# Hybrid decoder layer on one Trainium2 core: adaLN products as row products on VectorE, GpSimd and ScalarE, separate weight tiles for the output projection, and the next norm begun inside the input projection

## The chip, the cores and the metric

The kernel runs on one core of one Trainium2 chip. The metric is the device time of one execution in microseconds; for the kernel before it is the median of three runs. Engines are named as the profile names them: PE is TensorE's matmul and PEld its weight load, DVE is VectorE, ACT is ScalarE, POOL is GpSimd, SP is SyncE, whose queue issues nearly all DMAs of this kernel.

## The reference

One layer, batch 1, 2048 tokens, width 1024, all in float32:

```python
mod = jax.nn.silu(c) @ w_ada[layer] + b_ada[layer]
shift1, scale1, gate1, shift2, scale2, gate2 = jnp.split(mod, N_MOD, axis=-1)
h = modulate(rmsnorm(x, norm1_w[layer]), shift1, scale1)
x = x + gate1[:, None, :] * hybrid_mixer(h, ...)
h = modulate(rmsnorm(x, norm2_w[layer]), shift2, scale2)
x = x + gate2[:, None, :] * swiglu(h, w_gate_up[layer], w_down[layer])
...
return rmsnorm(x, final_norm_w)
```

`modulate(h, shift, scale)` is `h * (1 + scale) + shift`. `hybrid_mixer` makes one input projection (queries, keys, values, a gate z, the convolution's channels and dt), runs sliding-window attention on one half of the heads and a chunked state-space scan (SSD, 128 tokens in a chunk) on the other half, and joins both in one output projection. `w_ada` is 1024 x 6144; `mod` therefore has 48 groups of 128 numbers, and each group needs a 1024 x 128 piece of `w_ada`, 512 KB.

## The kernel before, in words

**Tiling.** Activations lie transposed: 128 channels on the partitions, 512 tokens along a row, so a block of 512 tokens is 8 tiles of 128x512. There are four blocks, 0 to 3. Every float32 matmul operand is split into a high and a low part of a faster format; `mm3` (lines 210 to 213) then issues three matmuls for each product. A weight tile is loaded by `weight` (lines 199 to 208): a DMA into one of five `raw` buffers, the high part by ACT (L204), the low part by POOL (L207) into one of six `w` pairs.

**Stages.** `first_norm` normalises block 0. Then, for each block b, `in_proj(b)` projects (queries, keys and values, eight convolution columns from `wx`, z), `norm1(b+1)` makes the operands of the next block, and for b = 1 and 2 `out_proj(b-1)` projects the mixer's output of the block before. Attention and SSD of a block are generators (`attentions`, `ssds`) that are kept in a list `sides`, and `beside` runs 1.6 steps of them for each step of the main generator. Before `out_proj(b-1)` stands `finish(ssd_of[b-1])`, which runs the list until that block's SSD is written: the output projection needs it. Attention of a block and its SSD follow each other, four steps of 128 tokens each, and the SSD carries a state from chunk to chunk. Later come the gate-up products of block pair 0 (`quads`, with a Strassen-like scheme of seven products), `down(0)` and `down(1)` with `out_proj(2)` and `out_proj(3)` beside them, the second pair's `quads`, and `down(2)` and `down(3)`.

**adaLN.** `ada(i, ...)` makes group i of `mod`. It loads 128x1024 numbers of `w_ada` (tile `mo` in the first norm, `aw` with a single buffer later) and issues eight matmuls (L142) that contract 128 input channels each with a column of silu(c) that is doubled to two columns (`csil`, 128x8x2). A matmul of this type is recorded as two weight loads and two passes, so eight matmuls are 16 records. DVE then adds the bias from PSUM. The first norm needs 16 groups (scale1 and shift1); `rest_of_ada` makes the other 32, one at each step of `beside` from `in_proj(1)` on. `first_norm` interleaves the groups with `modulated` (lines 242 to 248): DVE scales (L244), ACT makes the high part with the shift (L246), DVE the low part (L247); each of the eight results is one contraction step of the first queries' projection.

**Order.** The program is written as above, and a scheduler that estimates durations then orders the instructions of each engine. An engine takes its instructions strictly in that order; only the waits decide when each starts. SP's queue too is in order, so a DMA that waits for a free buffer holds the DMAs behind it.

**The final norm.** `down(b)` keeps eight residual tiles `x2` of its block (L807 loads them from `mid`), adds the products into them (L826), and leaves a generator that applies the final norm (L849, in place in `x2`) and stores (L850). It is run inside the next block's `down`, after columns 0 and 2. The residual tiles are a pool of eight, with three spare tiles `s` for even blocks.

## Time and profile before

| | |
|---|---|
| median of three runs | 2494.17 us (2491.22 to 2494.92) |
| the profiled execution | 2498.42 us, of which the span is 2496.6 us |
| mean granted TensorE clock | 0.958 |
| DVE, ACT, POOL busy | 55%, 42%, 58% of the span |
| DMA | 336.08 MB, mean 135 GB/s |

The chain that ended last lies on PE for 65% of the span, on DVE for 5%, on DMA for 2%. The program's stages, by the first and last instructions of their lines: first norm and queries of block 0 to 98.6 us, attention of block 0 from 120 to 305 us, its SSD to 408 us, `in_proj(1)` to 365 us, `out_proj(0)` from 395 us, attention of block 1 to 597 us and its SSD to 694 us, first `quads` from about 870 us, `down(0)` from about 1400 us, second `quads` from about 1750 us, `down(3)` from 2359 us to the end.

The views by stage give start:end, the length, then each engine's busy microseconds with its number of instructions, the granted clock, the DMA engines' busy share and GB/s. The timeline gives start, length, engine, line, operation, tiles, and in brackets the idle time before an instruction with what ended it. "Idle" in the groups' view is again time before the group's instructions, with the releaser behind it.

### The profile page before, as it was taken

To read this page: it belongs to the slowest core of one execution; us is meant where nothing else is said; L and a number is where in the kernel's file an instruction comes from. 1 tells how busy PE (TensorE), PEld (TensorE's weight loads), DVE (VectorE), ACT (ScalarE), POOL (GpSimd) and SP (SyncE) were. 2 spreads that over 40 slices of the span, in tenths; PEclk is the share of its full clock that TensorE was granted. 3 is DMA by queue.
4 is the path that set the end of the run, shared out by engine and by line. 5 is a ranking of instruction groups with operands and counts; after the bars stand their busy time and mean duration, and the time that the engine had idled before them with its cause. 6 is when DMAs were issued, how large, how long until landed. Compare 5 with 4: busy or idle time off the path is not lost.

```text
span 2496.6 us, 34763 instructions
## 1 busy us (share of the span) xinstructions
PE 2365.6 (95%) x11966; PEld 1995.6 (80%) x11966; DVE 1375.8 (55%) x2404; ACT 1060.5 (42%) x2155; POOL 1444.2 (58%) x1404
## 2 busy tenths in 40 slices
PE   7998998999689979999999999998999999999797
PEld 7988897899579858888888788876888888878576
DVE  5266455336644597665665535369555554554445
ACT  2366544446346643444443434334333333333332
POOL 2565563557546678655687544547666666643433
PEclk8899997999789979999999999999999999999998
DMA  6446555554444432222323555465242222263531
GB/s 217 130 150 192 180 175 176 193 171 146 125 156 148 130 107 91 81 73 85 99 87 95 180 172 187 154 222 162 89 141 76 81 86 87 76 198 101 186 117 61
DMA packets 208671, 336.08 MB, mean 135 GB/s; under 512 B 20592, under 2 KB 66672, under 8 KB 208496
## 3 DMA queue, kind: packets, MB, share of 16 engines
q1 hardware_dynamic: 207344, 332.83, 41.7%
q8 instruction: 94, 1.54, 0.3%
q10 hardware_dynamic: 1152, 1.05, 0.1%
q14 instruction: 81, 0.66, 0.1%
HBM read 266.69 MB, written 67.11 MB: 134 GB/s over the span
## 4 chain that ended last, share of the span: by engine, by line
PE 65%; DVE 5%; DMA 2%; issue 1%; ACT 1%; POOL 1%; SPq 0%; DVEq 0%; ACTq 0%
PE d L748 8%; PE d L746 8%; PE d L747 8%; PE d L211 8%; PE d L212 8%; PE d L213 8%; PE am L211 1%; PE am L213 1%; PE am L212 1%; PE am L748 1%; PE st L748 1%; PE sm L748 1%; PE sm L746 1%; PE am L746 1%; PE am L747 1%
## 5 line engine op out<-in xcount | busy, mean ns | idle before, releaser
L207 POOL TENSOR_TENSOR w<-raw,w 128x512 fp32r<-128x512 f32 (+1 forms) x224 | 295.9, 1327 | 255.4 <-ACT w L204 232.3
L692 ACT ACTIVATE w<-raw 128x512 fp32r<-128x512 f32 x308 | 193.6, 630 | 442.7 <-PE d L213 200.7
L747 PE MATMUL d<-b,w 128*128 128x512 f32 x924 | 368.2, 399 | 7.5 <-DVE b L720 7.1
L746 PE MATMUL d<-b,w 128*128 128x512 f32 x924 | 368.6, 399 | 0.3 <-DVE t L771 0.2
L748 PE MATMUL d<-b,w 128*128 128x512 f32 x924 | 367.9, 399 | 0.0
L211 PE MATMUL d<-a,w 128*128 128x512 f32 (+1 forms) x720 | 280.2, 396 | 28.2 <-DVE x L826 21.5
L212 PE MATMUL d<-a,w 128*128 128x512 f32 (+1 forms) x720 | 283.4, 394 | 4.4 <-DVE a L687 4.4
L213 PE MATMUL d<-a,w 128*128 128x512 f32 (+1 forms) x720 | 282.5, 392 | 0.0
L693 POOL TENSOR_TENSOR w<-s,w 128x512 fp32r<-128x512 f32 x132 | 189.4, 1435 | 156.8 <-ACT w L692 156.6
L693 POOL TENSOR_TENSOR w<-raw,w 128x512 fp32r<-128x512 f32 x88 | 123.4, 1403 | 197.3 <-ACT w L692 193.3
L693 DVE TENSOR_TENSOR w<-raw,w 128x512 fp32r<-128x512 f32 x220 | 191.6, 871 | 57.8 <-ACT w L692 52.3
L204 ACT ACTIVATE w<-raw 128x512 fp32r<-128x512 f32 (+1 forms) x224 | 139.8, 631 | 182.2 <-PE d L213 128.9
L747 PEld LDWEIGHTS d<-b,w 128*128 128x128 f32 x924 | 175.5, 190 | 47.9 <-DVE b L720 8.0
L746 PEld LDWEIGHTS d<-b,w 128*128 128x128 f32 x924 | 175.0, 189 | 40.4 <-DVE t L714 0.7
L826 DVE SCALAR_TENSOR_TENSOR x<-d,mod,x 128x512 f32<-128x512 f32 (+1 forms) x164 | 117.7, 722 | 162.5 <-PE d L213 150.4
L748 PEld LDWEIGHTS d<-b,w 128*128 128x128 f32 x924 | 175.0, 189 | 38.6
L211 PE MATMUL d<-w,hl 128*128 128x256 f32 (+1 forms) x640 | 187.6, 296 | 1.3 <-ACT hl L246 1.3
L212 PE MATMUL d<-w,hl 128*128 128x256 f32 (+1 forms) x640 | 187.6, 294 | 0.0
L213 PE MATMUL d<-w,hl 128*128 128x256 f32 (+1 forms) x640 | 187.1, 295 | 0.4 <-DVE hl L247 0.4
L211 PEld LDWEIGHTS d<-a,w 128*128 128x128 f32 x720 | 136.8, 190 | 62.3 <-issue 19.7
L212 PEld LDWEIGHTS d<-a,w 128*128 128x128 f32 x720 | 137.2, 191 | 37.4 <-DVE a L687 7.1
L213 PEld LDWEIGHTS d<-a,w 128*128 128x128 f32 x720 | 136.9, 190 | 31.5 <-issue 0.5
(312 smaller groups left out, 5654.4 us busy)
## 6 DMA issues: line engine op xcount, KB each, us to landing
raw<-in_wgu_dram SPq DMA_DIRECT2D x176, 256.0 KB, 2.7
raw<-in_wd_dram SPq DMA_DIRECT2D x176, 256.0 KB, 2.7
act<-t SPq DMA_DIRECT2D x88, 256.0 KB, 2.1
t<-act SPq DMA_DIRECT2D x88, 256.0 KB, 4.4
t<-in_xT_dram SPq DMA_DIRECT2D x80, 256.0 KB, 3.8
raw<-in_wx_dram SPq DMA_DIRECT2D x64, 256.0 KB, 3.0
aw<-in_wada_dram SPq DMA_DIRECT2D x32, 512.0 KB, 3.8
raw<-in_wo_dram SPq DMA_DIRECT2D x64, 256.0 KB, 2.7
```

The source lines that it names most:

```text
L204: nc.scalar.activation(hi, raw[:, :n], AF.Copy)
L207: eng.tensor_tensor(lo, raw[:, :n], hi.bitcast(F32), ALU.subtract)
L211: nc.tensor.matmul(out, ahi, bhi, start=first, stop=False)
L212: nc.tensor.matmul(out, ahi, blo, start=False, stop=False)
L213: mm3.last = nc.tensor.matmul(out, alo, bhi, start=False, stop=last)
L692: nc.scalar.activation(hi, x, AF.Copy)
L693: eng.tensor_tensor(lo, x, hi.bitcast(F32), ALU.subtract)
L746: nc.tensor.matmul(out, ahi, bhi, start=first and k == 0, stop=False, skip_group_check=True)
L747: nc.tensor.matmul(out, ahi, blo, start=False, stop=False, skip_group_check=True)
L748: mm3.last = nc.tensor.matmul(out, alo, bhi, start=False, stop=k == 3, skip_group_check=True)
L826: nc.vector.scalar_tensor_tensor(x, ps, gate2[:, c:c + 1], x, ALU.mult, ALU.add)
```

## The change

- `ada` no longer uses PE. `w_ada` is laid out with an output channel on each partition and the 1024 inputs along the row; silu(c), doubled, is broadcast to all partitions (`csil`, now 128x1024, from a new input `crow`). A group is then a product with `csil` and a sum along the row, half of which is taken (0.5). By default DVE does this in one instruction, `tensor_tensor_reduce`, that also adds the bias. For the eight shift groups of the first norm (`shared`) POOL multiplies (128x1024), ACT sums with its accumulator, and DVE adds the bias.
- `rest_of_ada` is started in step 4 of `in_proj(0)`, and not after it.
- `weight` takes an optional pool of its own: the output projection loads into two `rawo` buffers and two `wo` pairs instead of the five and six that all weights shared. A switch that shared the low parts with DVE (`share`) goes; nothing used it.
- `norm1(b+1)` is split: loads, squares, sum and reciprocal root come in step 4 of `in_proj(b)`, the spreading and `modulated` after it.
- In `down`, the final norm writes into a temporary tile and not in place, only block 0 uses the spare tiles `s`, and block 3 has eight residual tiles in a pool of its own, in the space that the second `quads`' operands leave.

```diff
...
@@ -128,18 +128,24 @@
         nc.gpsimd.memset(invf[:, j:j + 1], float(freqs[j]))
 
 
-    csil = const([P, 8, 2], "csil", pool=ip)
-    cth = const([P, 8], "cth", pool=ip)
-    nc.scalar.activation(cth, ccol, AF.Tanh, scale=0.5)
-    nc.vector.scalar_tensor_tensor(cth, cth, 1.0, ccol, ALU.add, ALU.mult)
-    nc.vector.tensor_scalar(csil, cth.unsqueeze(2).broadcast_to([P, 8, 2]), 0.5, None, ALU.mult)
+    csil = const([P, D], "csil", pool=ip)
+    nc.sync.dma_start(csil, crow.broadcast_to([P, D]))
+    for i in range(2):
+        cs, th = csil[:, i * T:(i + 1) * T], big("it", 3, pool=ip)
+        nc.scalar.activation(th, cs, AF.Tanh, scale=0.5)
+        nc.vector.scalar_tensor_tensor(cs, th, 1.0, cs, ALU.add, ALU.mult)
     mod = const([P, 48], "mod", pool=cst)
 
-    def ada(i, tag, bufs, out):
+    def ada(i, tag, bufs, shared=False):
         w = ip.tile([P, 2, T], F32, name=tag, tag=tag, bufs=bufs).rearrange("p h t -> p (h t)")
         load = nc.sync.dma_start(w, wada[i])
-        for k in range(KT):
-            nc.tensor.matmul(out, w[:, k * P:(k + 1) * P], csil[:, k, :], start=k == 0, stop=k == KT - 1)
+        m = mod[:, i:i + 1]
+        if shared:
+            nc.gpsimd.tensor_tensor(w, w, csil, ALU.mult)
+            nc.scalar.activation(w, w, AF.Copy, scale=0.5, accum_out=m)
+            nc.vector.tensor_tensor(m, m, b_ada[:, i:i + 1], ALU.add)
+        else:
+            nc.vector.tensor_tensor_reduce(w, w, csil, 0.5, b_ada[:, i:i + 1], ALU.mult, ALU.add, m)
         return load
 
     dsh = const([P, 4], "dsh", pool=cst)
@@ -194,17 +200,17 @@
         split.last = nc.vector.tensor_tensor(lo, x, hi.bitcast(F32), ALU.subtract)
         return hi, lo
 
-    turn = [0]
-
-    def weight(src, n=T, share=False):
-        raw = wt.tile([P, 528], F32, name="raw", tag="raw", bufs=RAW)
-        two = wt.tile([P, 2, 528], F32R, name="w", tag="w", bufs=SPLIT)
+    def weight(src, n=T, own=None):
+        if own is None:
+            raw = wt.tile([P, 528], F32, name="raw", tag="raw", bufs=RAW)
+            two = wt.tile([P, 2, 528], F32R, name="w", tag="w", bufs=SPLIT)
+        else:
+            raw = own.tile([P, T], F32, name="rawo", tag="rawo", bufs=2)
+            two = own.tile([P, 2, T], F32R, name="wo", tag="wo", bufs=2)
         hi, lo = two[:, 0, :n], two[:, 1, :n]
         nc.sync.dma_start(raw[:, :n], src)
         nc.scalar.activation(hi, raw[:, :n], AF.Copy)
-        turn[0] += share
-        eng = nc.vector if share and turn[0] % 3 == 0 else nc.gpsimd
-        eng.tensor_tensor(lo, raw[:, :n], hi.bitcast(F32), ALU.subtract)
+        nc.gpsimd.tensor_tensor(lo, raw[:, :n], hi.bitcast(F32), ALU.subtract)
         return hi, lo
 
     def mm3(out, ahi, alo, bhi, blo, first, last):
@@ -256,11 +262,12 @@
         acc = tmp()
         for d in range(KT):
             square_into(acc, load_x(b, d), d == 0)
-        yield
-        bc = spread(rstd(acc))
-        yield
+        y = rstd(acc)
+        yield
+        bc = spread(y)
         for d in range(KT):
             h.append(modulated(load_x(b, d), bc, scl1[:, d:d + 1], sh1[:, d:d + 1]))
+        yield
 
 
     q_d = [dr.tile([P, T], F32, name=f"q{t}") for t in range(S // P)]
@@ -662,7 +669,7 @@
         for c in range(KT):
             ps = bank_of(c)
             for half in range(2):
-                whi, wlo = weight(wo[c, half])
+                whi, wlo = weight(wo[c, half], own=pool)
                 for i in range(4):
                     k = 4 * half + i
                     ws = slice(i * P, (i + 1) * P)
@@ -797,13 +804,12 @@
 
     finish_of = {}
 
-    def down(b, dn):
+    def down(b, dn, x_pool):
         x2 = []
 
         def residual():
             c = len(x2)
-            extra = c < 3 and b % 2 == 0
-            x2.append(big("s", 3, pool=fw) if extra else big("x2", 8, pool=dn))
+            x2.append(big("s", 3, pool=fw) if c < 3 and b == 0 else big("x2", 8, pool=x_pool))
             nc.sync.dma_start(x2[c], mid[b][c])
         for g in range(6):
             n = G if g < 5 else NF - 5 * G
@@ -845,9 +851,9 @@
                     yield
                     bc = spread(y, bc=side_bank(3))
                     for d in range(KT):
-                        x = x2[d][:, ts]
-                        nc.vector.scalar_tensor_tensor(x, x, fw_[:, d:d + 1], bc, ALU.mult, ALU.mult)
-                        (nc.scalar if b == NB - 1 and d % 2 else nc.sync).dma_start(outT[b, d][:, ts], x)
+                        x, o = x2[d][:, ts], tmp()[:, ts]
+                        nc.vector.scalar_tensor_tensor(o, x, fw_[:, d:d + 1], bc, ALU.mult, ALU.mult)
+                        (nc.scalar if b == NB - 1 and d % 2 else nc.sync).dma_start(outT[b, d][:, ts], o)
                     yield
 
                 for part in range(parts):
@@ -881,15 +887,11 @@
         acc = accs[0]
         nc.vector.tensor_tensor(acc, acc, accs[1], ALU.add)
         bc = spread(rstd(acc, st=side_bank(0)), bc=side_bank(1))
-        ps = side_bank(3)
-        one = const([P, 8], "one", pool=ip)
-        nc.vector.tensor_scalar(one, b_ada[:, 8:16], 1.0, None, ALU.add)
         for d in range(KT):
-            for i in (8 + d, d):
-                load = ada(i, "mo", 8, ps[:, 2 * i:2 * i + 2])
-            nc.vector.scalar_tensor_tensor(scl1[:, d:d + 1], ps[:, 2 * (8 + d):2 * (8 + d) + 1], one[:, d:d + 1],
-                                           n1w[:, d:d + 1], ALU.add, ALU.mult)
-            nc.vector.tensor_tensor(sh1[:, d:d + 1], ps[:, 2 * d:2 * d + 1], b_ada[:, d:d + 1], ALU.add)
+            ada(8 + d, "mo", 8)
+            nc.vector.scalar_tensor_tensor(scl1[:, d:d + 1], mod[:, 8 + d:9 + d], 1.0, n1w[:, d:d + 1],
+                                           ALU.add, ALU.mult)
+            load = ada(d, "mo", 8, True)
             h.append(modulated(x0[d], bc, scl1[:, d:d + 1], sh1[:, d:d + 1]))
         return h, load
 
@@ -902,10 +904,8 @@
 
     def rest_of_ada(after_load):
         for i in (*range(16, 24), *range(32, 40), *range(24, 32), *range(40, 48)):
-            ps = dense()[:, 0:2]
             with tc.issue_after(after_load.ins):
-                ada(i, "aw", 1, ps)
-            nc.vector.tensor_tensor(mod[:, i:i + 1], ps[:, 0:1], b_ada[:, i:i + 1], ALU.add)
+                ada(i, "aw", 1)
             if i == 39:
                 nc.vector.scalar_tensor_tensor(scl2, mod[:, 32:40], 1.0, n2w, ALU.add, ALU.mult)
             if i == 31:
@@ -932,25 +932,23 @@
             if next(sides[0], sides) is sides:
                 sides.pop(0)
 
-    def project(b, h):
+    ssd_of = {}
+    for b in range(NB):
+        nxt = []
         for i in beside(in_proj(b, h), RATIO):
             if i == (2 if b == 0 else 3):
                 sides.append(attentions(b))
-        sd = ssds(b)
-        sides.append(sd)
-        return sd
-
-    ssd_of = {}
-    for b in range(NB):
-        ssd_of[b] = project(b, h)
+            if i == 4 and b + 1 < NB:
+                norm = norm1(b + 1, nxt)
+                with tc.issue_after(last_load.ins):
+                    next(norm)
+                if b == 0:
+                    ada_rest = rest_of_ada(load_x.last)
+        ssd_of[b] = ssds(b)
+        sides.append(ssd_of[b])
         if b + 1 < NB:
-            h = []
-            if b == 0:
-                with tc.issue_after(last_load.ins):
-                    drain(norm1(1, h))
-                ada_rest = rest_of_ada(load_x.last)
-            else:
-                drain(norm1(b + 1, h))
+            drain(norm)
+            h = nxt
         if b in (1, 2):
             finish(ssd_of[b - 1])
             drain(beside(out_proj(b - 1, y_of, ip, lambda c: dense()), RATIO))
@@ -971,22 +969,23 @@
     with tc.tile_pool(name="op", bufs=1, reuse_waits="tile") as op:
         for b in (2, 3):
             sides.append(out_proj(b, y_of, op, lambda c: side_bank(c % 2), lambda: side_bank(2)))
-        drain(beside(down(0, dn), 0.36))
-        rest = down(1, dn)
+        drain(beside(down(0, dn, dn), 0.36))
+        rest = down(1, dn, dn)
         for _ in beside(rest, 0.8):
             if not sides:
                 break
-    bp = ctx.enter_context(tc.tile_pool(name="b1", bufs=1, reuse_waits="tile"))
-    ops = {}
-    sides.append(operands(1, ops, bp, [side_bank(0), side_bank(1)]))
-    last = sides[-1]
-    drain(beside(rest, 0.25))
-    finish(last)
-    for i, _ in enumerate(quads(1, ops, lambda f: [side_bank(i) if f % 2 else dense() for i in range(4)])):
-        if i in (0, 2):
-            norm_of_block_before(2)
-    drain(down(2, dn))
-    drain(down(3, dn))
+    with tc.tile_pool(name="b1", bufs=1, reuse_waits="tile") as bp:
+        ops = {}
+        sides.append(operands(1, ops, bp, [side_bank(0), side_bank(1)]))
+        last = sides[-1]
+        drain(beside(rest, 0.25))
+        finish(last)
+        for i, _ in enumerate(quads(1, ops, lambda f: [side_bank(i) if f % 2 else dense() for i in range(4)])):
+            if i in (0, 2):
+                norm_of_block_before(2)
+    drain(down(2, dn, dn))
+    x3 = ctx.enter_context(tc.tile_pool(name="x3", bufs=1, reuse_waits="tile"))
+    drain(down(3, dn, x3))
 
 
 _OUTS = [((1, S, D), "float32")]
...
+    out["crow"] = a(c.reshape(1, D))
...
-    out["wada"] = a(w_ada[0].reshape(8, P, 48, P).transpose(2, 1, 0, 3).reshape(48, P, D))
+    out["wada"] = a(w_ada[0].T.reshape(48, P, D))
...
```

**The first norm.** On PE the kernel before had the 16 groups' matmuls (L142) between the norm's sum (L226), its spreading (L239) and the first products of the queries (L211 to L213):

```order
L142 MATMUL st<-csil,mo 128x2 x13
L226 MATMUL am<-ones,t 128x2 x4
L142 MATMUL st<-csil,mo 128x2 x17
L239 MATMUL at<-t,ones 128x512
L142 MATMUL st<-csil,mo 128x2 x18
L211 MATMUL d<-w,hl 128x256
L212 MATMUL d<-w,hl 128x256
L213 MATMUL d<-w,hl 128x256
```

In the changed kernel PE has none of them, and DVE has the scale groups' product and sum (L148, a main instruction and a read of the accumulator) among the operations that make `hl`; at this place its rows are:

```order
L148 ISA mo,mod<-mo,csil,vec 128x1024
L148 ISA mod 128x1
L250 SCALAR_TENSOR_TENSOR t<-mo,scl_147,at 128x512 x2
L892 SCALAR_TENSOR_TENSOR scl_147<-mod,vec 128x1
L250 SCALAR_TENSOR_TENSOR t<-mo,scl_147,at 128x512
L253 SCALAR_TENSOR_TENSOR hl<-t,mod,hl 128x512
```

The matmuls have moved off PE, and DVE's row of 1024 numbers now stands ahead of the scaling (L250, formerly L244) of the same channels.

**The end of the second input projection.** PE before, from the last group of `in_proj(1)` on (L590 to L629 are SSD, L226 and L239 the norm of block 2, L142 groups of `rest_of_ada`):

```order
L142 MATMUL d<-csil,aw 128x2 x8
L590 MATMUL sm<-m_3247,m_3366 128x64 x4
L590 MATMUL sm<-m_3247,m_3437 128x64 x4
L226 MATMUL d<-ones,t 128x2 x4
L629 MATMUL st<-ident,m_3163 128x128 x4
L597 MATMUL st<-state,m_3238 128x256 x2
L239 MATMUL d<-t,ones 128x512
```

PE now, at the same end (L217 to L219 are `mm3`, L559 to L636 SSD, `wo` the output projection's weights):

```order
L219 MATMUL d<-w,hl 128x256
L245 MATMUL d<-t,ones 128x512
L559 MATMUL st<-ident,m_2839 128x128 x4
L597 MATMUL sm<-m_2442,m_2621 128x64 x4
L597 MATMUL sm<-m_2442,m_2630 128x64 x4
L613 MATMUL sm<-m_2444,m_2451 128x256 x2
L566 MATMUL st<-ident,m_2839 128x128 x2
L571 MATMUL st<-m_2839 128x128 x2
```

A chunk ends with its transpositions at L629, now L636. Before, one chunk's stood ahead of the projection's last row and three behind it; now all four stand behind it, with 24 rows of the output projection among them. On DVE all 32 products of `rest_of_ada` stand ahead of the first SSD chunk.

**The last block's residuals.** SP before, at the start of `down(3)`: the stores of block 2 (L850), then five residual loads (L807) into tiles that those stores leave:

```order
L850 DMA out_dram<-x_20472 128x512
L850 DMA out_dram<-x_20493 128x512
L698 DMA raw<-in_wd_dram 128x512
L807 DMA x_21445<-mid_207 128x512
L807 DMA x_21466<-mid_207 128x512
L807 DMA x_21487<-mid_207 128x512
L807 DMA x_21508<-mid_207 128x512
L807 DMA x_21529<-mid_207 128x512
```

SP now, where `down(2)` has only begun, long ahead of any store of block 2:

```order
L819 DMA t<-act_217 128x512 x6
L813 DMA x_20967<-mid_210 128x512
L819 DMA t<-act_217 128x512
L813 DMA x_21008<-mid_210 128x512
L819 DMA t<-act_217 128x512
L813 DMA x_21029<-mid_210 128x512
L813 DMA x_21081<-mid_210 128x512
```

All eight residual loads of block 3 (L813, formerly L807) have moved ahead of the stores of block 2.

9 lines of the change are left out of this document (4 added, 5 removed).

## The prediction

> **What bounds the kernel now.** First the page's head and busy shares:
>
> ```profile
> span 2496.6 us, 34763 instructions
> PE 2365.6 (95%) x11966; PEld 1995.6 (80%) x11966; DVE 1375.8 (55%) x2404; ACT 1060.5 (42%) x2155; POOL 1444.2 (58%) x1404
> ```
>
> PE is busy for 95%, so work that leaves PE is worth its time, but only where PE ends last. Next the view by stages around the change, all engines:
>
> ```profile
> 125.00:300.00 175.00, 167.15 (x1137) 152.29 (x1136) 97.76 (x260) 112.72 (x260) 104.52 (x122) 0.99 0.54 172
> 365.00:408.00 43.00, 35.96 (x159) 30.46 (x159) 27.30 (x65) 17.77 (x43) 15.48 (x38) 0.64 0.55 177
> 408.00:470.00 62.00, 61.21 (x346) 52.87 (x345) 20.85 (x57) 27.18 (x63) 25.43 (x20) 0.97 0.59 200
> 470.00:600.00 130.00, 126.25 (x858) 117.26 (x858) 55.97 (x184) 78.17 (x181) 78.83 (x93) 0.96 0.50 159
> 600.00:694.00 94.00, 71.45 (x405) 59.62 (x405) 60.63 (x105) 36.52 (x87) 54.10 (x85) 0.82 0.43 132
> ```
>
> The first number behind the length is PE, then weight loads, DVE, ACT, POOL. Attention of block 0 (125 to 300) and the output projection with attention of block 1 (408 to 600) are PE's; in the stages 365 to 408 and 600 to 694 the clock granted is low and PE has holes: there SSD chunks follow one another. The same view for the adaLN matmuls alone (L142):
>
> ```profile
> 0.00:35.00 35.00, 16.66 (x76) 16.75 (x77) 1.00 0.77 267
> 35.00:86.00 51.00, 30.10 (x181) 30.53 (x181) 0.68 0.37 123
> 86.00:300.00 214.00, 17.05 (x145) 17.65 (x145) 0.97 0.53 169
> 300.00:365.00 65.00, 9.32 (x79) 9.82 (x79) 0.97 0.54 173
> 365.00:408.00 43.00, 7.80 (x51) 8.22 (x50) 0.64 0.55 177
> 408.00:600.00 192.00, 29.80 (x240) 30.50 (x240) 0.96 0.53 172
> sum 600.00, PE 110.73 PEld 113.47; mean PE 18.46 PEld 18.91
> ```
>
> So 110.7 us of PE is at stake, 30.1 us of it from 35 to 86 us, at a clock of 0.68, where the rest of PE is the queries. The timeline of PE then gives the ends that the sum needs: last query product, first and last transposition of block 0's attention, two ends of SSD chunks.
>
> ```profile
> 98.64 0.29 PE L213 MATMUL d<-w,hl 128*128 128x256 f32 x1
> 120.60 0.27 PE L453 MATMUL at<-ident,m 128*128 128x128 f32 x1
> 304.59 0.60 PE L526 MATMUL at<-ident,m 128*128 128x128 f32 x4
> 389.14 1.12 PE L629 MATMUL st<-ident,m 128*128 128x128 f32 x4 [2.26 <-DVE m L585]
> 407.92 0.60 PE L629 MATMUL st<-ident,m 128*128 128x128 f32 x4
> ```
>
> Attention of block 0 takes 184 us, its SSD 104 us, and the last chunk 19 us while PE has little else to do. Last, PE's waits from 2300 us on, and the stages around the longest:
>
> ```profile
> PE d L211 <- DVE x L826: 13.9, 1, 13.9
> ...
> 2360.00:2370.00 10.00, 0.00 (x0) 0.00 (x0) 4.07 (x7) 0.00 (x0) 0.58 (x1) 0.69 1.05 397
> 2370.00:2380.00 10.00, 6.86 (x21) 5.49 (x22) 4.86 (x7) 3.05 (x5) 2.32 (x2) 0.62 0.53 195
> ```
>
> PE stands still for 13.9 us while block 2's results are stored and block 3's residuals are read into the same tiles, and restarts at a clock of 0.62.
>
> **First norm and queries.** PE loses 256 records. What bounds then is the making of `hl`. Rows of the groups' view for the nearest operations:
>
> ```profile
> L503 DVE CUSTOM_DVE_ANT_0 m<-am,amask,row 128x256 f32<-128x256 f32 x120 | 53.1, 479 | 48.0 <-PE am L213 42.3 <-ACT m L520 5.7
> L503 DVE DVE_READ_ACCUMULATOR2_ANT ast<- 128x1 f32 x128 | 10.4, 81 | 0.0
> L247 DVE SCALAR_TENSOR_TENSOR hl<-t,mod,hl 128x512 fp32r<-128x512 f32 x32 | 26.2, 824 | 9.8 <-ACT hl L246 9.4
> L826 DVE SCALAR_TENSOR_TENSOR x<-d,mod,x 128x512 f32<-128x512 f32 x148 | 110.0, 747 | 159.2 <-PE d L213 147.1 <-DMA x<-mid 8.7 <-issue 3.4
> L207 POOL TENSOR_TENSOR w<-raw,w 128x512 fp32r<-128x512 f32 x192 | 253.7, 1328 | 226.2 <-ACT w L204 203.2 <-issue 17.2 <-DVE x L826 3.0
> L204 ACT ACTIVATE w<-raw 128x512 fp32r<-128x512 f32 x192 | 119.8, 629 | 161.4 <-PE d L213 111.1 <-PE am L213 11.0 <-issue 11.0
> ```
>
> `tensor_tensor_reduce` is L503's instruction at 256 numbers: 479 ns. From 256 to 512 numbers a DVE operation grows by 747 - 479 = 268 ns at most, so 1024 numbers take about 0.48 + 3 x 0.27 = 1.28 us, with the accumulator's read 1.36 us. POOL's product of 1024 is two of L207, 2.66 us; ACT's sum at most two of L204, 1.26 us. On POOL eight products (21.2 us), eight low parts of query weights (10.6 us), two of the output projection that its own tiles let come early (2.7 us) and two of keys (2.7 us) make 37 us; about 13 us of it can run before the norm is spread. How POOL and DVE meet is seen in the timeline:
>
> ```profile
> 8.04 0.69 DVE L166 SCALAR_TENSOR_TENSOR it<-it 128x512 f32<-128x512 f32 x1
> ...
> 10.24 2.96 POOL L221 TENSOR_TENSOR t<-t 128x512 f32<-128x512 f32 x2 [0.39 <-ACT t L220]
> 10.33 1.75 DVE L167 SCALAR_TENSOR_TENSOR it<-it 128x512 f32<-128x512 f32 x1
> ...
> 31.43 0.75 DVE L244 SCALAR_TENSOR_TENSOR t<-mo,scl,at 128x512 f32<-128x512 f32 x1 [2.17 <-PE at L239]
> ```
>
> The same DVE operation takes 0.69 us alone and 1.75 us beside POOL: it waits for about one POOL instruction. The spread norm is first used at 31.4 us, and I leave that. Behind it lie 24 us of POOL; if DVE hides wholly, queries end at 31 + 24 + 5 for the last step's 24 products, 60 us; if DVE's part (product 1.36, scaling 0.75, low part 0.82, two columns of 0.2, eight times: 27 us) only runs between POOL's, at 87 us. The middle, 73 us, is my value: a gain of 25 us (12 to 39). The transfers do not bind: a stage early on (the figure at its end is GB/s) shows what the DMA engines can move,
>
> ```profile
> 10.00:15.00 5.00, 2.83 (x14) 2.86 (x14) 5.00 (x6) 2.64 (x4) 2.88 (x2) 1.00 1.03 413
> ```
>
> about 400 GB/s, at which 14 MB (16 groups 8.4, x 2.1, query weights 2.1, `csil` 0.5, early weights of the output projection and the keys 1) take 35 us.
>
> **Attention and SSD of block 0.** The chain starts 25 us earlier. By the order, PE's rows between its first and last transposition lose 72 adaLN rows (144 records, 17 us) and gain 30 rows of 512 columns (0.23 us each) and 132 of 256 (0.12 us each), 23 us: it lasts 6 us longer. DVE takes 32 products there: 32 x 1.7 us (1.36 and a quarter of a POOL instruction) are 54 us on top of 97.8 us in 175 us. That still is less than PE's part, but DVE's queue is in order and each product waits there for its own load, so I put 10 us (0 to 30) on the attention chain. Then three of four chunks have nothing beside them: 25 us for the first and 3 x 21 us, 88 us in place of 104 us, 16 us gained. Net at the start of the output projection: 25 - 6 - 10 + 16 = 25 us. The 34 us of L142 from 86 to 408 us thus bring nothing by themselves; the SSD chain ends last.
>
> **Output projection and input projection 2.** From 408 to 600 us PE bounds, and 29.8 us of L142 go. I take 24 us (15 to 30), since attention of block 1 has waits of its own. Against it stand the two weight tiles: a load (2.7 us), ACT 0.63 and POOL 1.33 make 4.7 us for each, so two give one in 2.3 us, and 12 products want one in 12 x 0.23 = 2.8 us:
>
> ```profile
> raw<-in_wo_dram SPq DMA_DIRECT2D x64, 256.0 KB, 2.7
> ...
> 1433.00:1648.00 215.00, 215.00 (x936) 174.31 (x935) 90.43 (x138) 79.03 (x132) 113.22 (x86) 1.00 0.53 169
> ```
>
> That is hidden with little to spare; a queue of 0.3 us for each of the 32 half columns of blocks 0 and 1 costs 10 us (0 to 25). Beside `down(0)` and `down(1)`, the second row, 32 half columns take 215 us, 6.7 us each, and nothing is lost. The chunks of block 1 (600 to 694 us) stay as they are.
>
> **The end, and the edits at nothing.** With own residual tiles the 13.9 us go, and 2 us of slow clock: 16 us. The stores from temporary tiles free block 0's residuals earlier: 2 us. The earlier norm moves 8 loads, 8 squares and 7 sums of POOL (9 us) beside convolution columns, where PE covers them; without that cover they cost those 9 us. It brings nothing, since the SSD chain and not the norm ends `in_proj`.
>
> **Sum.** 25 + 24 - 10 + 16 + 2 = 57 us. The profiled execution took 2498.4 us (span 2496.6), 4 us above the median of the runs, 2494.2; from the median: 2437 us.
>
> **The rivals.** *All of it.* Every microsecond of L142 shows, and the end's 18: 2494 - 111 - 18 = 2365 us. For it speaks PE's 95%; against it the stages 365 to 408 and 600 to 694.
> *POOL holds DVE.* Each of the 32 products waits for a whole POOL instruction: 98 + 7 + 32 x (1.36 + 1.33) = 191 us, as much as PE needs, and the two no longer hide each other: 30 us of loss in place of 10, and with 25 in place of 10 at the output projection 2472 us. The Trainium skill says in "GPSIMD Engine Reference" (Specifications) that both engines share SBUF's interfaces, and contend where DVE has two inputs there; L167's row agrees.
> *DVE waits for loads (slower).* `aw` has one buffer, and a product that stands too early in DVE's queue holds attention's operations behind it. At one transfer and one product each,
>
> ```profile
> aw<-in_wada_dram SPq DMA_DIRECT2D x32, 512.0 KB, 3.8
> ```
>
> DVE needs 98 + 7 + 32 x (3.8 + 1.36) = 270 us, 80 us more than PE; the sum turns to 57 + 10 - 80 = -13, 2507 us. It decides from (190 + 67 - 105) / 32 = 4.75 us for a product with its wait. For it speaks that load and product alternate on one buffer, 5.2 us a pair, 32 times, in a stage of 175 us; against it that the scheduler sets the products apart.
>
> **Chances.** Forecast 0.48 (2410 to 2460); all of it 0.13 (2355 to 2400); POOL holds DVE 0.15 (2460 to 2488); DVE waits for loads 0.24 (2490 to 2540). The range 2390 to 2520 leaves out most of the second and two fifths of the last, 0.2 together. A measurement here tells about 0.2%, 5 us, from no change: faster 0.48 + 0.13 + 0.15 = 0.76; of the last case 0.04 is the same and 0.20 slower.
>
> **What would show it.** Queries end near 73 us; no L142 on PE; attention of block 0 ends near 290 us and its SSD near 383 us, with PE's clock low for some 60 us ahead; DVE in the attention stage between 75% and 90% busy; no wait of PE at the start of `down(3)`. Queries past 87 us, products on DVE that idle for their load by over 3 us each, or waits of PE for `wo` above 1 us each would make it wrong.

## The result: 0.9% slower, and the profile after

| | before | changed |
|---|---|---|
| median, same chip | 2493.24 us (4 runs) | 2514.91 us (4 runs, 2513.37 to 2523.12) |
| ratio, 95% interval | | 1.0094 (1.0071 to 1.0117) |
| span of the profiled execution | 2496.6 us | 2511.7 us |
| mean granted TensorE clock | 0.958 | 0.951 |

The forecast was 2437 us, so even the sign is wrong. The head of the changed kernel's page, then its view by stages, with the windows in which the prediction shows the kernel before (PE, PEld, DVE, ACT, POOL busy; clock, DMA share, GB/s):

```profile
span 2511.7 us, 33257 instructions
...
PE 2288.0 (91%) x11198; PEld 1899.1 (76%) x11198; DVE 1478.8 (59%) x2451; ACT 1063.3 (42%) x2172; POOL 1490.7 (59%) x1412
```

```profile
125.00:300.00 175.00, 141.53 (x865) 127.46 (x866) 130.43 (x299) 91.63 (x210) 99.75 (x102) 0.91 0.65 208
365.00:408.00 43.00, 28.48 (x106) 20.64 (x106) 30.69 (x48) 17.54 (x40) 21.23 (x37) 0.64 0.38 125
408.00:470.00 62.00, 48.54 (x198) 36.46 (x197) 25.77 (x60) 27.12 (x73) 22.30 (x40) 0.72 0.34 111
470.00:600.00 130.00, 126.41 (x781) 112.37 (x780) 64.16 (x194) 79.23 (x183) 85.25 (x97) 0.99 0.45 146
600.00:694.00 94.00, 72.50 (x421) 59.98 (x420) 64.44 (x96) 40.05 (x94) 59.98 (x89) 0.80 0.45 136
```

PE was relieved: it is busy 78 us less over the whole span. But the span grew by 15 us, so PE stands still 93 us longer. In the stage from 125 to 300 us PE is busy 141.5 us where it was busy 167.2 us, and DVE 130.4 us where it was 97.8 us. The later adaLN products all lie between 99 and 277 us, as the view of the tile `aw` shows (durations are minimum, median and maximum in ns, then the first and last start):

```profile
L148 DVE CUSTOM_DVE_ANT_0 aw<-aw,csil,vec x32: 1273/1316/2408, 98.7 to 276.5; 128x1024 f32<-128x1024 f32 x32
its engine sat idle before it (us, times) until:
  DMA aw<-in_wada_dram: 44.8, 27
```

So 32 products take 1.3 us each in the median (1.6 us on average, 50.8 us together, by the groups' view), start 5.7 us apart, and DVE stands still for 44.8 us of that with attention's instructions queued behind. Little of DVE is left: the view by stages for the stretch of the products (third engine: DVE) has it busy 128.1 of 179.3 us, and with the waits for `aw` that makes 173 us.

```profile
L148 DVE CUSTOM_DVE_ANT_0 aw<-aw,csil,vec 128x1024 f32<-128x1024 f32 x32 | 50.8, 1588 | 44.8 <-DMA aw<-in_wada_dram 44.8
98.70:278.00 179.30, 139.85 (x842) 125.33 (x843) 128.13 (x288) 87.49 (x204) 105.92 (x108) 0.91 0.68 220
```

The timeline of PE gives the milestones: the first keys' product, the first and last scores of attention 0, the last product with `later_r` of SSD(0) and of SSD(1) (called the end of an SSD from here on), and the last norm sum:

```profile
87.46 0.36 PE L217 MATMUL d<-w,hl 128*128 128x264 f32 x1 [0.19 <-DVE it L319]
...
131.89 0.28 PE L217 MATMUL am<-k_ring,m 128*128 128x256 f32 x1
...
321.09 0.28 PE L219 MATMUL am<-k_ring,m 128*128 128x256 f32 x1
...
417.12 0.63 PE L588 MATMUL sm<-m,later_r 128*128 128x512 f32 x1
...
673.81 0.40 PE L588 MATMUL sm<-m,later_r 128*128 128x512 f32 x1
...
2500.30 1.01 PE L232 MATMUL sm<-ones,t 128*128 128x2 f32 x4 [8.55 <-POOL t L227]
```

The same rows of the kernel before:

```profile
98.77 0.29 PE L211 MATMUL d<-w,hl 128*128 128x264 f32 x1
...
133.40 0.28 PE L211 MATMUL am<-k_ring,m 128*128 128x256 f32 x1
...
271.65 0.28 PE L213 MATMUL am<-k_ring,m 128*128 128x256 f32 x1
...
385.40 0.63 PE L581 MATMUL sm<-m,later_r 128*128 128x512 f32 x1
...
675.48 0.40 PE L581 MATMUL sm<-m,later_r 128*128 128x512 f32 x1
```

The keys come 11 us earlier, attention 0 takes 189 us for 138, SSD(0) ends 32 us late, SSD(1) on time, and what follows SSD(1) takes 1838 us for 1821. Two questions follow: where the gain ahead of SSD(1) went, and what the 17 us behind it are.

All kernels that were run, with these milestones in us from each profiled execution ("behind" is the span less the end of SSD(1)). Ratios are against the kernel before on the same chip.

| kernel | median | ratio (95%) | keys | attention 0 lasts | SSD(0) ends | SSD(1) ends | behind |
|---|---|---|---|---|---|---|---|
| before | 2493.2 | 1 | 99 | 138 | 385 | 675 | 1821 |
| changed | 2514.9 | 1.0094 (1.0071, 1.0117) | 87 | 189 | 417 | 674 | 1838 |
| p_ada | 2492.1 | 0.9993 (0.9982, 1.0005) | 82 | 165 | 409 | 671 | 1821 |
| p_own | 2501.9 | 1.0038 (1.0024, 1.0053) | 98 | 139 | 381 | 658 | 1842 |
| p_norm | 2503.5 | 1.0037 (1.0021, 1.0053) | 93 | 138 | 385 | 674 | 1821 |
| p_tail | 2498.0 | 1.0024 (1.0008, 1.0039) | 101 | 139 | 383 | 672 | 1829 |
| f_first | 2485.5 | 0.9968 (0.9952, 0.9985) | 83 | 139 | 371 | 662 | 1821 |
| f_rest | 2515.0 | 1.0099 (1.0078, 1.0119) | 106 | 154 | 421 | 692 | 1824 |
| f_aw4 | 2488.0 | 0.9976 (0.9960, 0.9992) | 83 | 160 | 396 | 664 | 1821 |
| f_dve16 | 2489.8 | 0.9985 (0.9971, 0.9999) | 70 | 163 | 398 | 672 | 1819 |
| n_early | 2489.1 | 0.9989 (0.9975, 1.0002) | 83 | 167 | 395 | 667 | 1820 |
| f_x3 | 2477.4 | 0.9940 (0.9919, 0.9961) | 96 | 139 | 383 | 668 | 1808 |
| x_noown | 2505.7 | 1.0046 (1.0030, 1.0063) | 83 | 180 | 413 | 678 | 1826 |
| x_nonorm | 2498.8 | 1.0027 (1.0014, 1.0040) | 88 | 168 | 404 | 660 | 1836 |
| x_inplace | 2508.5 | 1.0054 (1.0039, 1.0069) | 87 | 192 | 426 | 685 | 1820 |
| x_fixed | 2465.3 | 0.9884 (0.9869, 0.9899) | 70 | 158 | 391 | 659 | 1805 |
| c_first | 2455.9 | 0.9857 (0.9834, 0.9879) | 70 | 140 | 365 | 652 | 1804 |
| c_all | 2458.8 | 0.9875 (0.9854, 0.9897) | 70 | 155 | 384 | 652 | 1807 |
| c_paced | 2460.9 | 0.9860 (0.9831, 0.9890) | 70 | 155 | 372 | 655 | 1807 |
| c_mixp | 2453.8 | 0.9832 (0.9805, 0.9860) | 70 | 142 | 366 | 646 | 1809 |

One caution: before, p_tail and f_x3 are the same program up to SSD(1), and their profiles have it at 675, 672 and 668 us. A single milestone is good to some 7 us; verdicts below rest on the medians.

### The profile page after: what moved, and what is told of

Same layout as the page of the kernel before. It is cut to its first block, busy times and chain, and to the rows that moved or that the text cites. A ratio compares the mean times of both kernels' runs of the same rounds, so it can differ in the third digit from the quotient of the medians.

```text
span 2511.7 us, 33257 instructions
## 1 busy us (share of the span) xinstructions
PE 2288.0 (91%) x11198; PEld 1899.1 (76%) x11198; DVE 1478.8 (59%) x2451; ACT 1063.3 (42%) x2172; POOL 1490.7 (59%) x1412
## 4 chain that ended last, share of the span: by engine, by line
PE 62%; DVE 5%; POOL 2%; issue 1%; DMA 1%; ACT 1%; SPq 0%; DVEq 0%; POOLq 0%; ACTq 0%
PE d L755 8%; PE d L753 8%; PE d L754 8%; PE d L217 7%; PE d L218 7%; PE d L219 7%; PE am L217 1%; PE am L219 1%; PE am L218 1%; PE st L753 1%; PE st L755 1%; PE am L755 1%; PE am L754 1%; PE st L754 1%; PE am L753 1%
## 5 line engine op out<-in xcount | busy, mean ns | idle before, releaser
L217 PE MATMUL d<-a,w 128*128 128x512 f32 (+1 forms) x720 | 281.7, 398 | 18.3 <-DVE x L832 9.9
L213 POOL TENSOR_TENSOR w<-raw,w 128x512 fp32r<-128x512 f32 (+1 forms) x160 | 218.6, 1375 | 113.2 <-ACT w L212 97.5
L219 PE MATMUL d<-a,w 128*128 128x512 f32 (+1 forms) x720 | 281.7, 391 | 0.0
L832 DVE SCALAR_TENSOR_TENSOR x<-d,mod,x 128x512 f32<-128x512 f32 (+1 forms) x182 | 131.2, 724 | 167.3 <-PE d L219 163.7
L217 PE MATMUL d<-w,hl 128*128 128x256 f32 (+1 forms) x640 | 189.1, 298 | 27.2 <-ACT hl L252 17.5
L219 PE MATMUL d<-w,hl 128*128 128x256 f32 (+1 forms) x640 | 183.0, 297 | 1.8 <-DVE hl L253 1.8
L217 PEld LDWEIGHTS d<-a,w 128*128 128x128 f32 x720 | 136.8, 190 | 53.3 <-ACT a L821 11.6
L699 ACT ACTIVATE w<-s 128x512 fp32r<-128x512 f32 x176 | 110.1, 628 | 128.6 <-PE d L755 80.6
L219 PEld LDWEIGHTS d<-a,w 128*128 128x128 f32 x720 | 137.2, 191 | 31.6 <-issue 0.2
```

The source lines that it names most:

```text
L213: nc.gpsimd.tensor_tensor(lo, raw[:, :n], hi.bitcast(F32), ALU.subtract)
L217: nc.tensor.matmul(out, ahi, bhi, start=first, stop=False)
L219: mm3.last = nc.tensor.matmul(out, alo, bhi, start=False, stop=last)
L699: nc.scalar.activation(hi, x, AF.Copy)
L832: nc.vector.scalar_tensor_tensor(x, ps, gate2[:, c:c + 1], x, ALU.mult, ALU.add)
```

## The experiments

**One part of the change at a time, added to the kernel before.** *p_ada*: the adaLN products alone, the later ones begun after `in_proj(0)`.

```diff
-            nc.tensor.matmul(out, w[:, k * P:(k + 1) * P], csil[:, k, :], start=k == 0, stop=k == KT - 1)
+            nc.vector.tensor_tensor_reduce(w, w, csil, 0.5, b_ada[:, i:i + 1], ALU.mult, ALU.add, m)
```

> The kernel before with one part of the change: the adaLN products off TensorE (VectorE, and Pool with ACT for the eight first shifts), the 24 later groups begun where the kernel before begins them, after the first in_proj. Theory Q (the later products harm because they stand in VectorE's in-order queue ahead of what the first attention waits for, and wait there for loads into one buffer): here they fall beside SSD(0) and in_proj(1) and not beside attention(0), so attention(0) takes its 184 us again, most of the 12 us gained at the first queries and some of the 30 us of products on TensorE stay: 2455 to 2480. Rival P (the products on VectorE cost as much wherever they stand, since SSD hangs on VectorE as attention does): SSD(0) is stretched instead and the time is 2500 to 2520.

2492.14 us: no change. Neither range was met. The keys come 17 us earlier; at the end of SSD(1) 4 us of that are left, less than the scatter of a single profile.

*p_own*: the output projection's two weight tiles alone.

```diff
-                whi, wlo = weight(wo[c, half])
+                whi, wlo = weight(wo[c, half], own=pool)
```

> The kernel before with one part alone: two weight tiles of its own for the output projection (and every low part on Pool, as the changed kernel has it). Theory R (two pairs hold only the attention half of two output columns ahead of the SSD that is waited for, where six pairs held more): OUT(1), which had 48 rows before the end of SSD(1) and 24 after, ends some 15 us later and nothing gives it back: 2503 to 2515. Rival (the loss at OUT(1) of the changed kernel came from the other parts, and two pairs are refilled in time): 2489 to 2498.

8 us slower, just under the range of theory R. OUT(1) is `out_proj(1)`, and its sum is the norm's sum behind it. That sum is only 3 us late, but its SSD came 17 us sooner; from the end of SSD(1) to that sum the kernel before takes 70.5 us and p_own 91.2 us. The first row is the sum of the kernel before, whose end of SSD(1) is shown above; the other two are p_own's:

```profile
745.97 0.95 PE L226 MATMUL d<-ones,t 128*128 128x2 f32 x8
```

```profile
658.22 0.63 PE L581 MATMUL sm<-m,later_r 128*128 128x512 f32 x1
...
749.45 1.87 PE L226 MATMUL d<-ones,t 128*128 128x2 f32 x8 [2.08 <-POOL t L221]
```

Why SSD(1) came sooner in p_own was not tried.

*p_norm*: the early norm alone, with the later products on TensorE begun at step 4 too.

```diff
+            if i == 4 and b + 1 < NB:
+                norm = norm1(b + 1, nxt)
+                with tc.issue_after(last_load.ins):
+                    next(norm)
+                if b == 0:
+                    ada_rest = rest_of_ada(load_x.last)
```

> The kernel before with one part alone: squares and rstd of the next norm at step 4 of in_proj, and the later adaLN products, still on TensorE, begun there too. Theory Q says that the early place does harm only with the products on VectorE: within 5 us of the kernel before, 2488 to 2498. Rival N (it is the early norm and its eight loads that stretch attention(0), whatever engine has the products): 2505 to 2520. A third outcome, faster by 5 to 10 us, would be the spread and queries of the next block coming earlier.

9 us slower in the median, between the two ranges, and its runs scatter (2496.9 to 2511.7). The profiled one was the fastest of them and shows no loss. So that this pair of edits costs is measured; where it costs, and which of the two, the early norm or the early start of the later groups, is not.

*p_tail*: the last block's own residual pool, the final norm into temporary tiles, the spare tiles for block 0 only.

```diff
-                        x = x2[d][:, ts]
-                        nc.vector.scalar_tensor_tensor(x, x, fw_[:, d:d + 1], bc, ALU.mult, ALU.mult)
+                        x, o = x2[d][:, ts], tmp()[:, ts]
+                        nc.vector.scalar_tensor_tensor(o, x, fw_[:, d:d + 1], bc, ALU.mult, ALU.mult)
```

> The kernel before with one part alone: residuals of the last block in a pool of their own, the final norm's results into temp tiles. Theory E (9 us gained at the start of the last down, 8 us lost at the end since the last half's squares wait for temp tiles that the stores of the first half still read): 2489 to 2496, with a wait of TensorE of about 8 us for Pool before the last norm sum. Rival (the wait at the end comes from the other parts): 2476 to 2486.

4 us slower, a little above either range. PE's waits in p_tail, from 1650 to 1830 us and from 2300 us on (total, times, longest):

```profile
PE sm L226 <- POOL t L221: 4.7, 1, 4.7
PE d L748 <- DVE w L693: 3.0, 1, 3.0
```

```profile
PE sm L226 <- POOL t L221: 8.5, 1, 8.5
PE st L239 <- DVE t L237: 5.8, 2, 3.0
PE d L211 <- ACT a L814: 3.7, 3, 3.1
```

The 13.9 us at the start of `down(3)` are gone, but PE now waits for sums of squares (L221), whose tiles `t` are from the nine temporary ones. ACT's row for such a square shows what it waited for, the stores of the final norm's results:

```profile
2484.15 0.42 ACT L220 ACTIVATE t<-x 128x256 f32<-128x256 f32 x1 [10.84 <-DMA out_dram<-t]
```

The four parts alone add to 18 us (-2.2 + 7.5 + 9.2 + 3.7, each against the kernel before on its chip); the changed kernel lost 22 us.

**The end, without the temporary tiles.** *f_x3*: the kernel before with the residual pool alone.

```diff
-            x2.append(big("s", 3, pool=fw) if extra else big("x2", 8, pool=dn))
+            x2.append(big("s", 3, pool=fw) if c < 3 and b % 2 == 0 else big("x2", 8, pool=x_pool))
```

> The kernel before with the residual pool of the last block alone: the final norm stays in place (no temp tiles for its results), and block 2 keeps its three other tiles. Theory E2 (p_tail gained 12.6 us at the start of the last down and gave back 5 to 8 us in each of three places where the final norm takes eight of the nine temp tiles: in down(1), at the start of quads(1), at the end): all three losses are gone, 2478 to 2485. Rival (the wait at the start of the last down only moves to the next thing that is late): 2489 to 2496.

16.4 us faster, a little better than theory E2's range. Its waits from 2300 us on, with neither the 13.9 nor the 8.5 us:

```profile
PE st L239 <- DVE t L237: 9.3, 2, 5.6
PE d L211 <- ACT a L814: 3.2, 1, 3.2
```

**The halves of the adaLN part.** *f_first*: the first norm's 16 groups off TensorE, the 32 later ones on it as before. *f_rest*: the reverse. *f_aw4*: p_ada with `ada(i, "aw", 4)`. *f_dve16*: p_ada with `ada(d, "mo", 8)`, so no product on POOL. *n_early*: p_ada with the later groups begun at step 4 of `in_proj(0)`, without the early norm.

> The ada part alone as in p_ada, but the 32 later groups stay on TensorE as in the kernel before: only the first norm's 16 groups are off it. Theory Q: attention(0) starts at about 116 us (133 before) and, with no product in VectorE's queue, takes the 139 us of the kernel before where p_ada took 166; SSD(0) ends near 368 (385 before, 409 in p_ada), and 8 to 17 us of that reach the end: 2477 to 2486. Rival (what the first norm gains is lost at a later wait whatever stands in VectorE's queue, since p_ada lost all of it): 2490 to 2498.

> The other half of the ada part: the first norm on TensorE as in the kernel before, the 32 later groups on VectorE with one weight buffer, begun where the kernel before begins them. Theory Q: the two halves add to what p_ada measured (2 us faster, f_first 8 us faster), so this half alone is 4 to 10 us slower, 2497 to 2505, with SSD(0) ending 15 to 25 us after the 385 us of the kernel before, though TensorE has 30 us less to do. Rival (TensorE's relief is worth something by itself): 2484 to 2492.

> p_ada with four buffers for the later weight groups in place of one. Theory W (the harm of the later products is VectorE standing still for their loads, 50.8 us of it between 100 and 420 us in p_ada): those waits go to under 10 us, SSD(0) ends at 385 to 392 (409 in p_ada) and the time is 2474 to 2484. Rival V (the harm is the 32 products themselves, 1.3 us each in front of the side work, and the loads' share of the DMA engines): SSD(0) ends after 400, 2488 to 2496.

> p_ada with the eight shifts of the first norm on VectorE too, none on Pool and ACT. Theory T (Pool's 1024-wide products hold VectorE's two-input operations, so that the first norm gains 17 us and not 25): the first query products start by 34 us (42 in p_ada) and the keys by 76 (82), 2484 to 2490. Rival (VectorE is short of time there, and eight more products of 1.3 us cost 10 us): keys from 86 on, 2494 to 2502.

> p_ada with the 32 later groups begun at step 4 of the first in_proj, as in the changed kernel, without the early norm. Theory Q: now all of attention(0) has products and their loads in front of it on VectorE; it takes 180 to 195 us (166 in p_ada, 139 before), SSD(0) ends at 412 to 420 and the time is 2494 to 2504. Rival (the place does not matter, since the side work is served in turn): within 3 us of p_ada, 2489 to 2495.

f_first came as theory Q said: attention 0 takes 139 us again, SSD(0) ends at 371 us, and the kernel is 8 us faster. f_rest lost 22 us, more than either theory allowed: its keys are 7 us late as well (PE waits 14.2 us for a load of `mo`; whether the broadcast row on the DMA queues causes that was not tried), and attention 0 and what follows it to the end of SSD(0) are stretched by 16 and 15 us. So the later products, not the first norm's, take the gain back. f_aw4 lies between its theories: the waits are gone, as W said, but the time is V's. The `aw` views of p_ada and of f_aw4, the products and DVE's idle time before them:

```profile
L148 DVE CUSTOM_DVE_ANT_0 aw<-aw,csil,vec x32: 1273/1346/2440, 200.4 to 387.5; 128x1024 f32<-128x1024 f32 x32
...
  DMA aw<-in_wada_dram: 50.8, 24
```

```profile
L148 DVE CUSTOM_DVE_ANT_0 aw<-aw,csil,vec x32: 1267/1494/2393, 201.1 to 291.0; 128x1024 f32<-128x1024 f32 x32
...
  DMA aw<-in_wada_dram: 3.3, 3
```

The waits go from 50.8 to 3.3 us, SSD(0) ends 13 us sooner and the time falls by 4 us. But most of the stretch stays: from the keys to the end of SSD(0) f_first, with the later groups on PE, takes 287 us, p_ada 328 and f_aw4 313. So the waits for loads are about a third of the 41 us, and two thirds stay with the 32 products themselves. n_early refutes theory Q's point about the place: an early start costs nothing by itself (3 us less than p_ada, the intervals overlap). f_dve16 has the keys 12 us earlier, as theory T said, but not the first product of the queries, which stays at 42 us where T said 34. Though the later products took most of the gain back, it is 2 us under p_ada (the intervals overlap) and not above it.

**Parts taken out of the changed kernel.** *x_noown* goes back to the shared weight ring, *x_nonorm* to the undivided norm (the later products still begin at step 4), *x_inplace* to the final norm in place with block 2's spare tiles. *x_fixed* keeps the early norm and mends the rest: four `aw` buffers, no product on POOL, shared ring, norm in place.

> The changed kernel without its own weight tiles for the output projection (the shared ring, and the low parts dealt as before). Theory R, as the runs so far leave it (with two pairs OUT(1) ends 87 to 95 us after SSD(1), with the ring 71 to 74): OUT(1)'s last sum comes 73 us after SSD(1) ends near 673, at about 746 (760 in the changed kernel), attention(0) and SSD(0) stay as they are (417), and the time is 2500 to 2508. Rival (OUT(1) is late because SSD(0) was late, not for want of tiles): 2511 to 2516.

> The changed kernel without the early norm; the 32 later groups begin at step 4 all the same. Theory N (the early norm's loads and squares and the products together stretch attention(0) to 189 us, where each alone left 139 and 167): attention(0) takes 165 to 172 us, SSD(0) ends at 395 to 400 (417), and the time is 2500 to 2508. Rival (the products' place does it): SSD(0) after 410, 2510 to 2516.

> The changed kernel with the final norm in place and block 2's three other tiles kept, the last block's residual pool kept. Theory E2 (the temp tiles cost 5 us in down(1), 6 at the start of quads(1), 7 at the end): 2494 to 2502, and the wait of TensorE for Pool before the last norm sum (8.5 us) is gone. Rival: 2508 to 2515.

> The changed kernel with its early norm and with the four other things mended: four buffers for the later weights, no product on Pool, the shared weight ring, the final norm in place. The difference to c_all (2458.8, the same without the early norm) is the early norm's price: by theory N 5 to 15 us, 2464 to 2474; by the rival (the early norm costs nothing once the products' loads are ahead) 2455 to 2462.

x_noown: 9 us come back, and OUT(1)'s sum follows SSD(1) by 71.9 us in place of 86.3. Theory R expected that, but not that attention 0 would take 180 us in place of 189, the keys coming 5 us sooner. x_nonorm: 16 us come back, 1 us more than theory N allowed, and attention 0 takes 168 us in place of 189, as it said, though SSD(0) is a little later. But without the early norm's loads ahead of theirs the products also begin at 75 us in place of 99, and PE stands still in attention 0 nearly as long as in the changed kernel (30 us for 32). So what the early norm does itself and what it does by pushing the products further into attention is not separated. x_inplace: the stretch behind SSD(1) is 18 us shorter in the profile, and the wait of 8.5 us is gone, but the median fell by only 6.5 us, to 2508.5 us, in the rival's range; its profile has 11 us more ahead of SSD(1), where both kernels are the same program, so the size of this part inside the changed kernel stays open. x_fixed is 28.7 us under the kernel before and 6.5 us above c_all, in the range of theory N. It does not show the early norm's price, though: the intervals of the two ratios overlap, and c_all, unlike what the expectation says, is not the same without the early norm, since its later products begin at 190 us and those of x_fixed at 83 us.

Together with f_x3 these runs also divide the 17 us behind SSD(1), as far as single profiles go: the stretch is 12 us shorter without the two weight tiles (x_noown), 18 us shorter without the temporary tiles and with block 2's spare tiles (x_inplace), and the residual pool had taken 13 us off (f_x3).

**Versions put together.** *c_first*: first norm on DVE alone, later groups on TensorE, residual pool with the norm in place. *c_all*: the later groups on DVE too, with four buffers. *c_paced*: c_all with each later product held behind the newest DVE instruction of its step. *c_mixp*: c_first with the last 16 groups on DVE, held in the same way, and four `aw` buffers.

```diff
+            traced = nc.cur_bb.bb.instructions
+            newest = next(t for t in reversed(traced) if t.engine == in_proj.last.ins.engine)
+            with tc.issue_after(after_load.ins), tc.issue_after(newest):
+                ada(i, "aw", 4)
```

> Three parts that measured faster, together: the first norm's 16 groups on VectorE alone (none on Pool), the 32 later groups on TensorE as before, and the last block's residual pool with the final norm in place. If they add: f_first 8 us, f_x3 16 us, and of the 12 us that the keys come earlier without Pool's products the greater part, 2459 to 2470. Rival (a later wait takes the 12 us of the keys, as SSD(1) took the gains of p_ada): 2470 to 2476.

> As c_first, but the 32 later groups on VectorE too, with four buffers for their weights. If VectorE's later products cost nothing once their loads are ahead, it is no slower than c_first. Theory V (each product still stands in front of the side work of attention(0) and SSD(0)): SSD(0) ends 15 us or more after that of c_first, and the time is 3 to 12 us above it.

> c_all with each later product held in VectorE's issue order behind the newest VectorE instruction of its own step, so that they lie one to a step from the second in_proj to the third (some 190 to 550 us), where TensorE had them in the kernel before, and not all between 190 and 280 us. Theory B (what harms is that nothing holds the products on VectorE, so that all 32 bunch into some 90 to 180 us of attention(0) and SSD(0)): SSD(0) ends at 365 to 375 (384 in c_all, 365 in c_first), the 30 us off TensorE tell between SSD(0) and SSD(1), and the time is 2440 to 2453, under c_first (2455.9). Rival V (a product in front of the side work costs the same wherever it stands): 2455 to 2462.

> c_first with the last 16 of the later groups on VectorE, held back in the same way, so that they lie beside OUT(0) and the third in_proj, where VectorE is busy 37 to 44% of the time; the first 16 stay on TensorE. Theory B: SSD(0) ends at 365 as in c_first, SSD(1) up to 15 us sooner than its 652, 2441 to 2453. Rival (SSD(1) is bound by its own chain of VectorE, ACT and Pool there, and TensorE's 16 us of relief are worth nothing): 2453 to 2458.

c_first is 37 us faster than the kernel before, 3 us better than the range said for parts that add. c_all has SSD(0) 19 us later and SSD(1) at the same time:

```profile
364.80 0.63 PE L599 MATMUL sm<-m,later_r 128*128 128x512 f32 x1
...
651.54 0.40 PE L599 MATMUL sm<-m,later_r 128*128 128x512 f32 x1
```

```profile
383.93 0.39 PE L587 MATMUL sm<-m,later_r 128*128 128x512 f32 x1
...
651.67 0.63 PE L587 MATMUL sm<-m,later_r 128*128 128x512 f32 x1
```

The first pair is c_first, the second c_all. What 32 products cost on DVE ahead of SSD(0), the relief of TensorE brings back between SSD(0) and SSD(1): an exchange at par. c_paced spreads the products from 200 to 535 us; SSD(0) then ends 12 us sooner, as theory B said, but SSD(1) 3 us later, and the time is in the rival's range: a product in front of the side work costs about the same wherever it stands. c_mixp is 2 us under c_first, in the rival's range, and four runs of each cannot tell the two apart. Both beat both kernels.

## Why the prediction was wrong, by its own steps

**First norm and queries** (gain 25, range 12 to 39; last query product at 73 us). Measured 12: the keys start at 87 us. From the first scaling (L250) to there 44 us pass, as forecast (42). But the first scaling is at 43.4 us, and the step that failed is "The spread norm is first used at 31.4 us, and I leave that". The scalings of the changed kernel, of p_ada and of f_dve16 (durations, first and last start):

```profile
L250 DVE SCALAR_TENSOR_TENSOR t<-mo,scl,at x8: 742/747/750, 43.4 to 75.0; 128x512 f32<-128x512 f32 x8
```

```profile
L250 DVE SCALAR_TENSOR_TENSOR t<-mo,scl,at x8: 742/748/750, 40.7 to 72.1; 128x512 f32<-128x512 f32 x8
```

```profile
L250 DVE SCALAR_TENSOR_TENSOR t<-mo,scl,at x8: 729/743/748, 40.8 to 62.1; 128x512 f32<-128x512 f32 x8
```

With no product on POOL (f_dve16) the first scaling is as late as in p_ada: there, by DVE's timeline, eight of its own products stand in its queue ahead of it, among the norm's last operations. From there on POOL's products set the pace: to the keys p_ada needs 41 us and f_dve16 29. The two weight tiles add some 5 us: the keys come at 87 to 88 us in the three kernels that have them beside the products on POOL, and at 82 to 83 us in the five that have those products without them. How POOL holds DVE, the changed kernel's timelines of DVE and POOL show:

```profile
16.65 2.82 DVE L227 TENSOR_TENSOR t<-t 128x512 f32<-128x512 f32 x1
19.39 2.82 DVE L174 SCALAR_TENSOR_TENSOR it<-it 128x512 f32<-128x512 f32 x1
...
26.56 2.28 DVE L148 CUSTOM_DVE_ANT_0 mo<-mo,csil,vec 128x1024 f32<-128x1024 f32 x1
...
33.20 0.16 DVE L194 SCALAR_TENSOR_TENSOR rsq<-rsq,ms 128x4 f32<-128x4 f32 x1
...
33.79 1.27 DVE L194 SCALAR_TENSOR_TENSOR rsq<-rsq,ms 128x4 f32<-128x4 f32 x1
...
36.31 4.96 DVE L243 TENSOR_SCALAR t<-ident,rstd 128x128 f32<-128x128 f32 x4
```

```profile
16.14 5.53 POOL L144 TENSOR_TENSOR mo<-mo,csil 128x1024 f32<-128x1024 f32 x2
...
33.77 2.49 POOL L213 TENSOR_TENSOR w<-raw,w 128x512 fp32r<-128x512 f32 x2 [3.80 <-ACT w L212]
36.22 2.48 POOL L213 TENSOR_TENSOR wo<-rawo,wo 128x512 fp32r<-128x512 f32 x2
38.66 2.34 POOL L144 TENSOR_TENSOR mo<-mo,csil 128x1024 f32<-128x1024 f32 x1
```

L174 takes 2.82 us beside two products where it takes 0.69 us alone, and an operation on 128x4 numbers 1.27 us for 0.16. The latter stands beside a low part of a weight (L213), not beside a product, and in the kernel before the same operations take 1.13 to 1.21 us beside such low parts; L243 meets the low parts of `wo`, which the two tiles let come this early, and one product. The rival *POOL holds DVE* had this mechanism, but I put its price on the later products. The Trainium skill's page "SBUF — State Buffer" (Who interferes with whom) says that a DVE instruction with two SBUF inputs contends with a GpSimd instruction that reads SBUF. The rows of L227, L174 and L194 agree.

**Attention and SSD of block 0** (chain 16 us longer, SSD 16 us shorter, 25 us gained). This is the step that broke the forecast. The SSD's part was right (86 us from the last transposition of attention to that of SSD(0), forecast 88). But the attention chain became 49 us longer, not 16, and SSD(0) ended 32 us later than before, not 25 us earlier. The view by stages for PE, from the first to the last transposition of attention 0, before and changed:

```profile
120.60:304.60 184.00, 176.15 (x1176) 0.99 0.55 173
116.70:350.10 233.40, 196.95 (x1201) 0.93 0.61 195
```

PE is busy 21 us more, not 6, though its rows are nearly those that were counted; they ran at a granted clock of 0.93 in place of 0.99. And it stands still for 36 us in place of 8. The words that failed are "That still is less than PE's part, but DVE's queue is in order and each product waits there for its own load, so I put 10 us (0 to 30)". The products' 54 us were right (50.8), but the waits for loads came on top (44.8 us), and then DVE, not PE, was the engine with no time to spare. The runs divide the stretch of attention 0, 51 us by its scores: the products with one weight buffer 27 us (165 in p_ada, 167 in n_early, against 138), the early norm, with the products that it pushes back, 21 us (168 without it, 189 with it). The waits are the smaller part of what the products cost, by f_aw4 about a third.

This is the mechanism of the rival *DVE waits for loads*, but not its size. It had load and product alternate at 5.2 us a pair (5.7 measured), and took DVE as held for all of that; in fact DVE did 2.4 us of other work between two products (128.1 less 50.8 us, over 32). A product with its wait cost DVE 3.0 us (50.8 and 44.8 us over 32), which is under the 4.75 us from which the rival was to decide; and the sign that I had named, over 3 us of idle time for a product, was not reached either (1.7 us, 27 times). That its 2507 us lie near the measured time is in part luck, since the early norm and the temporary tiles, which it did not price, are in the measured time. I gave it 0.24 for "the scheduler sets the products apart"; the profile of before could not show that, since there the products were on PE.

**Output and input projection 2** (24 us gained). The size was about right: from SSD(0) to SSD(1) the kernel before takes 290 us, the changed one 257, and p_ada, f_aw4 and n_early 262 to 273. It was wrong to add it to an undisturbed SSD(0): it only paid back what the products had cost there. c_all has the 32 later groups off PE (64 us in the kernel before, by the last four rows of the L142 view in the prediction), c_first has them on it, and SSD(1) ends at the same time. The Trainium skill's "Perfetto Trace Analysis" (Identifying the Most-Contended Engine) says to optimize the engine with the highest occupancy first, and to judge TensorE's headroom by its weight loads among other things. By either share PE is the busiest engine of the kernel before (95%, weight loads 80%). Still, following the rule gained nothing in this stretch: relieving PE brought 19 us there, and the queue of the engine that took the work had lost as many before.

**The two weight tiles** (10 us lost, 0 to 25). Measured 8 alone and 9 taken out: right in size, by luck, for the mechanism was another. There is no queue at each half column: all of PE's waits for `wo` in p_own make 4 us. Two tiles let fewer products of OUT(1) run ahead of the end of SSD(1) (none of 192 in p_own, 22 in the changed kernel, 48 with the ring), and more of them are left after it: 85 to 91 us where the ring leaves 70 to 73.

**The end** (18 us gained). The 16 us for own residual tiles were exact (f_x3, 16.4). The 2 us for temporary tiles had the wrong sign: with them, and with block 2's spare tiles gone, p_tail is 20 us above f_x3 (the two edits were not tried apart). The prediction had asked only when residual tiles come free, and not who else draws on the nine temporary ones; the new waits are for squares in them.

**The edits at nothing.** The early norm was to be covered by PE, and to cost 9 us without that cover. Taken out of the changed kernel it gives 16 us back, and p_norm, which has it with the later groups on TensorE, is 9 us slower. So the cover failed, or the early start that comes with it cost; these runs do not show which, nor what the norm waits for there.
